# Gate and forget-group weights split during the first feed-forward, a longer reckoned load, and two token blocks per bank

## The chip, the cores and the metric

The kernel runs on one core of a Trainium2 chip. The metric is the device time of one execution in microseconds (us), from three runs of each kernel. The engines are named as the profile names them: PE (TensorE matmul), PEld (TensorE weight load), DVE (VectorE), ACT (ScalarE), POOL (GpSimd) and SP (SyncE, whose queue issues every DMA of this kernel).

## The reference, cut to what matters

One layer on 1024 tokens of width 1024, all in float32: a SwiGLU feed-forward, a mixer of two attentions side by side with sigmoid gates, and a second feed-forward, each behind an RMS norm with a shift, a scale and a gate from a conditioning vector.

```
h = modulate(x, norm_g[l, 0], mod[:, 0, 0], mod[:, 0, 1])
x = x + 0.5 * mod[:, 0, 2][:, None, :] * swiglu(h, ffn1_w1[l], ffn1_w3[l], ffn1_w2[l])
h = modulate(x, norm_g[l, 1], mod[:, 1, 0], mod[:, 1, 1])
# mixer: z = h @ w_in is split into
(fq, fk, fv, ff, dq, dk, dv, iq, ik, iw, ga, gb) = jnp.split(z, split_points, axis=-1)
# FoX: 8 heads, causal softmax with a forget bias; DSA: each query sees its 256 best keys by an index score
merged = jax.nn.sigmoid(ga) * (ya @ w_br_fox) + jax.nn.sigmoid(gb) * (yb @ w_br_dsa)
x = x + mod[:, 1, 2][:, None, :] * (merged @ w_out)
h = modulate(x, norm_g[l, 2], mod[:, 2, 0], mod[:, 2, 1])
x = x + 0.5 * mod[:, 2, 2][:, None, :] * swiglu(h, ffn2_w1[l], ffn2_w3[l], ffn2_w2[l])
```

## The kernel before

**Split operands.** Each float32 operand is split into a high part (ACT copies it to the matmul's type, tile `wh` for weights, `h` for activations) and a low part (the raw tile minus the high part, `wl`), and each product is three matmuls (`mm3`). In the feed-forwards DVE makes the low parts of the weights, as halves of 128x512. In the mixer `load_w` (line 565) loads a raw weight tile `wr` of up to 128x1024, ACT makes `wh`, and POOL (`k.lo_eng`, line 1981) makes `wl`.

**The stages, by the span of the profile.** The first feed-forward's up half (`up_all`, eleven pairs of column blocks, some 130 steps of twelve matmuls) ends near 470 us and its down half near 690; the normed `h` and the index, key and value projections follow; from 705 to 840 the index scores and the first two forget groups of the FoX attention (`fox_group`: query, key and value of two heads). From 840 to 1045 PE computes, one after the other, forget group 2, some gate columns, forget group 3, gates, the query groups `dq_group` 0, gates, `dq_group` 1 and the rest of the gates, while DVE and ACT run `topk` beside it: a search bit by bit for each query's 256th best score, with counts on DVE (`tkj`) and sign tests on ACT (`tks`), each depending on the last. From 1045 to 1405 the attentions run, with the gates of the second token half and the first branch products as filler. From 1405 on come branches, output projection and the second feed-forward, until 2229.

**The gates.** `gates` (line 1072) takes the 16 weight tiles `w_g[b]` (128x1024) for one half of the tokens; it runs twice, so each tile is loaded, copied by ACT and subtracted by POOL twice. `Ahead` (line 1054) holds the weights loaded in advance, three tiles in the stage from 840, one later. Their buffers come from `Ring`s: five pairs `wh`/`wl` and three raw tiles, and in the attentions two pairs and two raw tiles.

**The wide groups.** Forget groups 2 and 3 and both query groups run `group` with `wide`: weight tile by weight tile, and within each over all eight token blocks of 128, so eight accumulations are open at once, each in its own PSUM bank. `chain8` (line 62) deals these banks: four halves of the two 128x1024 tiles `p2`, then four tiles `pj`. The gates use the same four `pj`. At the end of a group ACT copies each block out (`qkv<-p`, `qkv<-pj`), 128x384 for a forget group and 128x256 for a query group.

**What sets the order.** `Plan` records each stage's instructions and `flush` writes them out engine by engine, by reckoned start times: each engine takes, of its ready tasks, the one that can start first, by rank. A task that is meant to fill gaps gets its rank raised (`nc.behind`). A load is reckoned to be there 0.7 us after its bytes are through the wire (lines 394 and 395):

```
self.wire = max(self.wire, s + 1.3) + t.bytes / 345e3
end = self.wire + 0.7
```

On the chip each engine then runs its own instructions strictly in that order.

Of the kernel before, what the change touches and what calls it, by code (L numbers as in the profile page):

```python
# [204 lines left out]
class Plan:  # L205
# [116 lines left out]
    def flush(self, keep=()):  # L322
# [42 lines left out]
        while len(order) < len(tasks):  # L365
# [180 lines left out]
class Ring:  # L546
# [416 lines left out]
def group(k, src, n, ptile, wide, done, weight=1.9):  # L963


    if not wide:
# [8 lines left out]
    ps = []  # L975
    for i in range(4):
        hi, lo = next(src)
        for tk in range(8):
            if i == 0:
                ps.append(ptile())  # L980
            hf, o = tk // 4, (tk % 4) * 128
            for c in range(2):
                hh, hl = (t[hf][2 * i + c][:, o:o + 128] for t in (k.hh, k.hl))
                cs = slice(c * n, c * n + n)
                mm3(k, ps[tk][:, :n], hh, hl, hi[:, cs], lo[:, cs], i + c == 0, i == 3 and c == 1)
            if i == 3:
                done(tk, ps[tk])
# [13 lines left out]
def norm_group(k, p, tmp, src, n, ptile, wide, weight=1.9):  # L1001
# [4 lines left out]
    def done(tk, ps):  # L1006
        k.nc.scalar.activation(t[tk // 4][:, tk % 4, :], ps[:, :n], AF.Copy)
# [934 lines left out]
def layer(tc, xT, c, pos, ada_w, ada_b, ng, inv, w13a, w2a, w_a, w_f, w_q, w_g, fb, fg, dg, wbr, wout, w13b, w2b, out):  # L1942
    with ExitStack() as es:
# [38 lines left out]
        dram = lambda shape, nm: dp.tile(shape, F32, name=nm)  # L1982
# [16 lines left out]
        with ExitStack() as ph:  # L1999
# [24 lines left out]
            def consts():  # L2024
# [15 lines left out]
                yield  # L2040

# [78 lines left out]
            for i in range(2, head):  # L2120
# [3 lines left out]
                if i == 4:  # L2124
# [12 lines left out]
            rest = up_all(k, pairs, head, [], {2: [more], 4: [more], 6: [more]}, lambda: down.loads(down.LEAD), chain(consts(), rest),  # L2137
                          (nc.vector, nc.vector), True, lambda n: n % 2)
            steps = {(5, 4): [lambda: stats(0)]}
# [7 lines left out]
            for q in range(4 * PAIRS):  # L2147
                steps.setdefault(divmod(q, PAIRS), []).append(more_mod)
            down.run(steps)
            assert next(rest, None) is None  # L2150
# [51 lines left out]
        with ExitStack() as ph:  # L2202
# [16 lines left out]
            for i, (w, n) in enumerate(((w_f[2], 768), (w_f[3], 768), (w_q[0], 512), (w_q[1], 512))):  # L2219
                parts += [(w[j], n, r5) for j in range(4)] + [(w_g[b], D, r5) for b in range(3 * i, 3 * i + 3)]  # L2220
            ws = Ahead(k, parts + [(w_g[b], D, r5) for b in range(12, 16)] + [(w_g[b], D, r2) for b in range(2)], 3)
# [5 lines left out]
        with ExitStack() as ph:  # L2227
            tp = pool(ph, "topk", True)
            pj = lambda: pq.tile([128, H], F32, tag="pj", name="pj", bufs=4)
            bank8 = chain8(pj, p2)  # L2230
            gt = gates(k, ws, 0, tp, pj, 2)
# [178 lines left out]
```

## Time and profile before

| | us |
|---|---|
| three runs, median (lowest to highest) | 2230.95 (2229.25 to 2231.05) |
| the profiled execution | 2230.78 |
| its span, first to last instruction | 2229.0 |
| PE busy | 2166.7 (97%) |
| DVE busy | 1638.6 (74%) |
| ACT busy | 1145.2 (51%) |
| POOL busy | 252.0 (11%) |

The profiled execution lies 1.8 us above its span. PE's busy time is modelled; a matmul of 128x512 takes its turn every 0.233 us when nothing holds it. The granted TensorE clock is 0.994 of full speed over the span, the rest lies in a few short stretches at half. DMA moved 315.88 MB, at a mean of 142 GB/s.

### The profile page before, as it was taken

To read this page: it belongs to the slowest core of one execution; us is meant where nothing else is said; L and a number is where in the kernel's file an instruction comes from. 1 tells how busy PE (TensorE), PEld (TensorE's weight loads), DVE (VectorE), ACT (ScalarE), POOL (GpSimd) and SP (SyncE) were. 2 spreads that over 40 slices of the span, in tenths; PEclk is the share of its full clock that TensorE was granted. 3 is DMA by queue.
4 is the path that set the end of the run, shared out by engine and by line. 5 is a ranking of instruction groups with operands and counts; after the bars stand their busy time and mean duration, and the time that the engine had idled before them with its cause. 6 is when DMAs were issued, how large, how long until landed. Compare 5 with 4: busy or idle time off the path is not lost.

```text
span 2229.0 us, 31185 instructions
## 1 busy us (share of the span) xinstructions
PE 2166.7 (97%) x10700; PEld 1782.9 (80%) x10700; DVE 1638.6 (74%) x3095; ACT 1145.2 (51%) x2105; POOL 252.0 (11%) x225
## 2 busy tenths in 40 slices
PE   7999999999999999989999998999999999999999
PEld 5877788887889899977777777777778888888887
DVE  7968776688684698888887677498865755558665
ACT  5634433444464566787777677244443333334443
POOL 0000000000010222223445343000000000000000
PEclk9999999999999999999999999999999999999999
DMA  9245543695421323235232212596224443258520
GB/s 333 95 149 178 173 152 109 213 351 195 125 89 57 109 78 130 96 123 161 90 120 88 72 39 81 202 354 189 66 81 132 137 130 103 96 207 287 166 76 38
DMA packets 186267, 315.88 MB, mean 142 GB/s; under 512 B 27238, under 2 KB 51814, under 8 KB 186108
## 3 DMA queue, kind: packets, MB, share of 16 engines
q1 hardware_dynamic: 186108, 313.89, 42.4%
q8 instruction: 84, 1.38, 0.3%
q14 instruction: 75, 0.61, 0.1%
HBM read 237.53 MB, written 76.28 MB: 141 GB/s over the span
## 4 chain that ended last, share of the span: by engine, by line
PE 82%; DVE 8%; ACT 5%; DMA 3%; issue 2%; SPq 0%; POOL 0%; DVEq 0%; ACTq 0%; POOLq 0%
PE bs L425 34%; PE b L425 28%; PE py L425 7%; PE pj L425 6%; PE p L425 5%; PE pt L425 2%; DVE qkv L425 1%; ACT tks L425 1%; DVE xc L425 1%; DMA mraw<-in_ada_w 1%; DMA wr<-in_w_f 1%; ACT pth L425 1%; ACT pr L425 1%; ACT wh L425 1%; DVE wl L425 1%
## 5 line engine op out<-in xcount | busy, mean ns | idle before, releaser
L425 PE MATMUL bs<-h,wh 128*128 128x512 f32 x1728 | 543.0, 395 | 1.6 <-ACT bs L425 1.3
L425 ACT ACTIVATE wh<-wr 128x512 fp32r<-128x512 f32 (+2 forms) x366 | 246.5, 679 | 451.7 <-PE bs L425 208.3
L425 PEld LDWEIGHTS bs<-h,wh 128*128 128x128 f32 x1728 | 322.9, 188 | 81.9 <-ACT bs L425 5.7
L425 PE MATMUL b<-h,wh 128*128 128x512 f32 x1088 | 344.8, 397 | 5.7 <-ACT z L425 2.6
L425 PE MATMUL bs<-h,wl 128*128 128x512 f32 x864 | 338.7, 393 | 0.5 <-DVE wl L425 0.5
L425 DVE TENSOR_TENSOR wl<-wr,wh 128x512 fp32r<-128x512 f32 x308 | 205.4, 686 | 123.5 <-ACT wh L425 116.6
L425 PEld LDWEIGHTS b<-h,wh 128*128 128x128 f32 x1088 | 205.0, 189 | 55.5 <-ACT z L425 3.5
L425 PE MATMUL b<-h,wl 128*128 128x512 f32 x544 | 214.7, 395 | 0.1
L425 PEld LDWEIGHTS bs<-h,wl 128*128 128x128 f32 x864 | 162.2, 188 | 39.2 <-DVE wl L425 0.9
L425 ACT ACTIVATE wh<-a 128x512 fp32r<-128x512 f32 x132 | 83.3, 631 | 174.4 <-PE b L425 93.0
L425 POOL TENSOR_TENSOR wl<-wr,wh 128x1024 fp32r<-128x1024 f32 (+2 forms) x58 | 123.8, 2137 | 328.6 <-ACT wh L425 323.3
L425 DVE TENSOR_TENSOR wl<-a,wh 128x512 fp32r<-128x512 f32 x132 | 91.3, 692 | 88.1 <-ACT wh L425 83.5
L425 PE MATMUL b<-wh 128*128 128x512 f32 x352 | 137.2, 390 | 0.7 <-ACT mrow L425 0.7
L425 PE MATMUL b<-wh,wl 128*128 128x512 f32 x352 | 137.0, 389 | 0.0
L425 PE MATMUL b<-wl,wh 128*128 128x512 f32 x352 | 137.0, 389 | 0.0
L425 PE MATMUL pj<-wh,h 128*128 128x384 f32 (+1 forms) x512 | 125.8, 324 | 0.3 <-ACT wh L425 0.2
L425 PEld LDWEIGHTS b<-h,wl 128*128 128x128 f32 x544 | 102.8, 189 | 25.1 <-DVE wl L425 0.7
L425 DVE TENSOR_TENSOR z<-bs,z 128x512 f32<-128x512 f32 x116 | 79.3, 687 | 58.7 <-PE bs L425 36.8
L425 POOL TENSOR_SCALAR pr<-pr,mn 128x128 f32<-128x128 f32 (+7 forms) x128 | 100.0, 801 | 134.7 <-DVE mn L425 127.5
L425 DVE TENSOR_TENSOR wl<-g,wh 128x512 fp32r<-128x512 f32 x154 | 106.5, 694 | 2.5 <-ACT wh L425 2.5
L425 ACT ACTIVATE pr<-pr,mn 128x256 f32<-128x256 f32 (+7 forms) x128 | 98.4, 770 | 18.0 <-DVE mn L425 17.7
L425 PE MATMUL bs<-wl,wh 128*128 128x512 f32 x264 | 103.1, 391 | 2.1 <-DVE wl L425 1.9
(322 smaller groups left out, 4405.2 us busy)
## 6 DMA issues: line engine op xcount, KB each, us to landing
d_g<-z SPq DMA_DIRECT2D x154, 256.0 KB, 2.1
g<-d_g SPq DMA_DIRECT2D x154, 256.0 KB, 4.7
mraw<-in_ada_w SPq DMA_DIRECT2D x144, 256.0 KB, 5.3
wr<-in_w13a SPq DMA_DIRECT2D x112, 256.0 KB, 5.3
wr<-in_w13b SPq DMA_DIRECT2D x88, 256.0 KB, 4.6
wr<-in_w_g SPq DMA_DIRECT2D x32, 512.0 KB, 4.2
a<-in_w2a SPq DMA_DIRECT2D x44, 256.0 KB, 5.1
a<-in_w2b SPq DMA_DIRECT2D x44, 256.0 KB, 5.3
```

Of the source, the lines that this page charges most:

```text
L425: getattr(getattr(self.tc.nc, e), t.op)(*map(real, t.a), **{n: real(v) for n, v in t.kw.items()})
```

## The change

1. `parts()`, new in the first feed-forward: 40 pieces (four weight tiles of forget group 2 in halves of 128x384, the 16 gate tiles in halves of 128x512). For each piece, one DMA loads it (`gw`), ACT makes the high part, POOL the low part, and two DMAs write both parts to DRAM (`d_wf..`, `d_wg..`). The 80 half-steps are hung on `up_all`'s steps 30 to 125, with ranks raised by 200.
2. Where the mixer needs these weights, `load_w` loads the high and the low part straight into the pair `wh`, `wl`: two DMAs, no raw tile, no ACT, no POOL. This holds for forget group 2 and for the gates, both times. Pairs are now dealt in turn.
3. The planner reckons a load 1.0 us longer.
4. `dq_group` takes its banks from `chain4`: only the four halves of the two `p2` tiles. Two token blocks of 256 columns share a bank, so a group has four accumulations of 128x512 and four copies out instead of eight.

```diff
+def chain4(two):
+    while True:
+        t = two()
+        yield t[:, 0:H]
+        yield t[:, H:T]
...
-                end = self.wire + 0.7
+                end = self.wire + 1.7
...
-        return tuple(p.tile([128, D], F32R, tag=t, name=t, bufs=n) for t in ("wh", "wl"))
+        return tuple(p.tile([128, D], F32R, tag=t, name=t, bufs=n, in_turn=True) for t in ("wh", "wl"))
...
+    if isinstance(src, tuple):
+        t = k.w.pair()
+        for part, d in zip(t, src):
+            nc.sync.dma_start(part[:, :n].bitcast(F32), d)
+        return t
...
-    ps = []
+    ps, m = [], H // n
...
-            if i == 0:
+            if i == 0 and tk % m == 0:
                 ps.append(ptile())
...
-                mm3(k, ps[tk][:, :n], hh, hl, hi[:, cs], lo[:, cs], i + c == 0, i == 3 and c == 1)
-            if i == 3:
-                done(tk, ps[tk])
+                mm3(k, ps[tk // m][:, tk % m * n:tk % m * n + n], hh, hl, hi[:, cs], lo[:, cs], i + c == 0,
+                    i == 3 and c == 1, tk % m > 0)
+            if i == 3 and tk % m == m - 1:
+                done(tk, ps[tk // m])
...
+            def parts():
+                for src, dst in todo:
+                    n = dst[0].shape[1]
+                    m = n if n <= H else n // 2
+                    for c in range(0, n, m):
+                        nc.behind = 200
+                        t, hi, lo = (t512(k, dt, "gw")[:, :m] for dt in (F32, F32R, F32R))
+                        nc.sync.dma_start(t, src[:, c:c + m])
+                        nc.scalar.activation(hi, t, AF.Copy)
+                        nc.gpsimd.tensor_sub(lo, t, hi.bitcast(F32))
...
+                        for d, x in zip(dst, (hi, lo)):
+                            nc.sync.dma_start(d[:, c:c + m], x.bitcast(F32))
...
+            for n in range(80):
+                steps.setdefault(30 + 96 * n // 80, []).append(lambda: next(gw, None))
...
-                       dq_group(k, fp, fp, tp, ws, 0, lambda: next(bank8), 0.8), islice(gt, 15),
-                       dq_group(k, fp, fp, tp, ws, 1, lambda: next(bank8), 0.6), gt)
+                       dq_group(k, fp, fp, tp, ws, 0, lambda: next(bank4), 0.8), islice(gt, 15),
+                       dq_group(k, fp, fp, tp, ws, 1, lambda: next(bank4), 0.6), gt)
```

In the order of the program, the kernel before: PE where query group 0 ends and the gates follow. `pj` on the left is a bank that is written, `wh,h` its weight and activation operands; `p_9157` and `p_9163` are the two `p2` tiles of query group 1.

```order
L425 MATMUL pj<-wl,h 128x256
L425 MATMUL pj<-wh,h 128x256
L425 MATMUL p_9157<-wh,h 128x256 x2
L425 MATMUL p_9163<-wh,h 128x256 x2
L425 MATMUL pj<-h,wh 128x512 x2
L425 MATMUL pj<-h,wl 128x512
```

The same place in the changed kernel; `p_9305` is the second `p2` tile of query group 0.

```order
L433 MATMUL p_9305<-wh,h 128x256 x2
L433 MATMUL p_9305<-wl,h 128x256
L433 MATMUL p_9305<-wh,h 128x256
L433 MATMUL pj<-h,wh 128x512 x2
L433 MATMUL pj<-h,wl 128x512
```

The gates' first bank (`pj<-h,wh 128x512`) no longer is a bank that the query group has just filled, and the four early matmuls of the next group have gone from between.

ACT at that place, before: the sign tests (`tks`) and the copies out of query group 0.

```order
L425 ACTIVATE qkv<-p_8674 128x256
L425 ACTIVATE tks,tksgn<-tkh_7948,tkca 128x896
L425 ACTIVATE qkv<-p_8674 128x256
L425 ACTIVATE tks,tksgn<-tkh_7920,tkca 128x768
L425 ACTIVATE fsq<-qkv 128x512
L425 ACTIVATE qkv<-p_8872 128x256 x2
L425 ACTIVATE qkv<-pj 128x256 x4
```

And in the changed kernel:

```order
L433 ACTIVATE qkv<-p_9086 128x512
L433 ACTIVATE tks,tksgn<-tkl_8308,tkca 128x768
L433 ACTIVATE fsq<-qkv 128x512
L433 ACTIVATE qkv<-p_9086 128x512
L433 ACTIVATE tks,tksgn<-tkl_8370,tkca 128x1024
L433 ACTIVATE qkv<-p_9305 128x512
L433 ACTIVATE tks,tksgn<-tkl_8338,tkca 128x896
L433 ACTIVATE fsq<-qkv 128x512
```

Sign tests still stand between the copies, but no copy out of a `pj` is left among them.

SP in the first feed-forward, before: the loads of one pair's weights (`wr`) between those for the conditioning rows (`mraw`); `d_g` is a store of the feed-forward.

```order
L425 DMA mraw<-in_ada_w 128x512 x2
L425 DMA d_g_120<-z 128x512
L425 DMA mraw<-in_ada_w 128x512 x2
L425 DMA wr<-in_w13a 128x512 x2
L425 DMA mraw<-in_ada_w 128x512
L425 DMA wr<-in_w13a 128x512 x2
```

The same four `wr` loads in the changed kernel and what now stands ahead of them (`gw` is a piece, `d_wg3h` and the like are the parts written out):

```order
L433 DMA d_wg3l<-gw 128x512
L433 DMA d_wg3h<-gw 128x512
L433 DMA mraw<-in_ada_w 128x512
L433 DMA d_wg3l<-gw 128x512
L433 DMA mcol<-d_row_163 128x4x1
L433 DMA d_wg4h<-gw 128x512
L433 DMA d_wg4l<-gw 128x512
L433 DMA gw<-in_w_g 128x512
L433 DMA d_g_200<-z 128x512
L433 DMA d_wg4h<-gw 128x512
L433 DMA wr<-in_w13a 128x512 x4
```

The four loads have moved behind stores that wait for ACT and POOL.

## Rows read from the trace of the kernel before

**Rows 1.** The page's first part: busy us, share of the span, instructions.

```profile
PE 2166.7 (97%) x10700; PEld 1782.9 (80%) x10700; DVE 1638.6 (74%) x3095; ACT 1145.2 (51%) x2105; POOL 252.0 (11%) x225
```

**Rows 2.** Windows by stage: stretch, us; PE, PEld, DVE, ACT, POOL busy; clock, DMA share, GB/s.

```profile
195.00:490.00 295.00, 294.03 (x1267) 235.87 (x1266) 215.14 (x342) 114.90 (x200) 0.00 (x0) 1.00 0.58 195
705.00:840.00 135.00, 127.30 (x726) 121.54 (x724) 90.94 (x160) 71.54 (x121) 31.72 (x24) 1.00 0.28 90
840.00:1045.00 205.00, 197.21 (x1108) 176.30 (x1108) 170.06 (x505) 159.30 (x293) 56.16 (x28) 0.98 0.37 118
1045.00:1405.00 360.00, 342.64 (x2346) 273.87 (x2345) 275.59 (x609) 255.49 (x557) 151.93 (x157) 0.98 0.30 93
```

**Rows 3.** Waits of PE: engine and tile, what it waited for, us, times, longest.

```profile
PE p L425 <- ACT ir L425: 4.6, 4, 1.9
PE p L425 <- ACT qkv L425: 4.3, 5, 1.5
PE pj L425 <- ACT qkv L425: 3.5, 1, 3.5
...
PE pt L425 <- DMA nat<-d_qkv: 1.3, 1, 1.3
```

**Rows 4.** Timeline of PE: start, us, instruction, [idle before <-releaser].

```profile
949.07 0.50 PE L425 MATMUL p<-wh,h 128*128 128x256 f32 x2 [1.05 <-ACT qkv L425]
951.05 0.51 PE L425 MATMUL p<-wh,h 128*128 128x256 f32 x2 [1.48 <-ACT qkv L425]
...
995.58 0.72 PE L425 MATMUL pj<-h,wh 128*128 128x512 f32 x2 [3.52 <-ACT qkv L425]
```

**Rows 5.** Timeline of ACT, 993 to 996 us.

```profile
994.01 1.15 ACT L425 ACTIVATE tks<-tkl,tkca 128x1024 bf16<-128x1024 uint16 x1
...
995.14 0.39 ACT L425 ACTIVATE qkv<-pj 128x256 f32<-128x256 f32 x1
```

**Rows 6.** Windows as in group 2, of shorter stretches.

```profile
230.00:260.00 30.00, 29.71 (x127) 23.38 (x126) 27.96 (x45) 12.12 (x21) 0.00 (x0) 1.00 0.51 167
430.00:510.00 80.00, 79.32 (x346) 64.22 (x345) 62.76 (x103) 37.65 (x67) 0.00 (x0) 1.00 0.96 339
946.00:956.00 10.00, 7.47 (x35) 6.11 (x34) 7.64 (x21) 9.69 (x22) 1.39 (x2) 0.83 0.16 50
990.00:1000.00 10.00, 6.48 (x30) 5.38 (x29) 8.32 (x31) 10.00 (x24) 1.83 (x2) 0.83 0.66 201
```

**Rows 7.** Timeline of DVE and of POOL near 932 us.

```profile
932.04 0.15 DVE L425 TENSOR_TENSOR tku<-tkcnt,tklim 128x3 uint32<-128x3 f32 x1
932.23 2.26 DVE L425 SCALAR_TENSOR_TENSOR tkkey<-tku,tkkey 128x3 uint32<-128x3 uint32 x1
...
932.07 2.40 POOL L425 TENSOR_TENSOR wl<-wr,wh 128x1024 fp32r<-128x1024 f32 x1 [3.16 <-ACT wh L425]
```

**Rows 8.** Groups of DVE, 840 to 1045 us: xcount | busy, mean ns | idle before.

```profile
L425 DVE TENSOR_TENSOR qkv<-qkv,fnr 128x1024 f32<-128x1024 f32 x10 | 16.0, 1643 | 0.1
L425 DVE TENSOR_TENSOR tku<-tkcnt,tklim 128x3 uint32<-128x3 f32 x32 | 11.7, 365 | 0.8
L425 DVE TENSOR_TENSOR tkv<-tksgn,tklim 128x3 f32<-128x3 f32 x31 | 11.2, 361 | 19.8 <-ACT tks L425 19.7
L425 DVE TENSOR_TENSOR qkv<-qkv,g_dq 128x1024 f32<-128x1024 f32 x4 | 4.9, 1216 | 0.0
```

**Rows 9.** Groups of POOL, 840 to 1045 us.

```profile
L425 POOL TENSOR_TENSOR wl<-wr,wh 128x1024 fp32r<-128x1024 f32 x16 | 38.5, 2404 | 95.0 <-ACT wh L425 95.0
L425 POOL TENSOR_TENSOR wl<-wr,wh 128x512 fp32r<-128x512 f32 x8 | 10.3, 1292 | 45.3 <-ACT wh L425 45.3
```

**Rows 10.** Groups of ACT: the first of 195 to 490 us, the second of 840 to 1045.

```profile
L425 ACT ACTIVATE wh<-wr 128x512 fp32r<-128x512 f32 x76 | 47.7, 630 | 111.7 <-PE bs L425 63.9 <-PE b L425 35.0 <-issue 6.6
...
L425 ACT ACTIVATE wh<-wr 128x1024 fp32r<-128x1024 f32 x16 | 16.9, 1054 | 10.9 <-issue 10.9
```

**Rows 11.** Page, DMA issues: count, KB each, median us from issue to landing.

```profile
wr<-in_w_g SPq DMA_DIRECT2D x32, 512.0 KB, 4.2
```

More of the change, by code (lines that the diff above doesn't have):

```diff
@@ L1006, in done @@
     def done(tk, ps):
-        k.nc.scalar.activation(t[tk // 4][:, tk % 4, :], ps[:, :n], AF.Copy)
+        m = H // n if wide else 1
+        k.nc.scalar.activation(t[tk // 4][:, tk % 4 - m + 1:tk % 4 + 1, :], ps[:, :m * n].rearrange("p (a b) -> p a b", a=m),
+                               AF.Copy)
         if tk % 2:
@@ L1981, in layer @@
         k.lo_eng = nc.gpsimd
-        dram = lambda shape, nm: dp.tile(shape, F32, name=nm)
+        dram = lambda shape, nm, dt=F32: dp.tile(shape, dt, name=nm)
+        split_in = lambda n, m, nm: [tuple(dram([128, m], f"d_{nm}{i}{x}") for x in "hl") for i in range(n)]
+        d_wg = split_in(16, D, "wg")
+        d_wf = [split_in(4, 768, f"wf{i}") for i in range(4)]
+        d_wq = [split_in(4, 512, f"wq{i}") for i in range(2)]
+        todo = [(w[i], d[i]) for w, d in (((w_f[2], d_wf[2]), (w_g, d_wg))) for i in range(len(d))]
         d_x = dram([8, 128, T], "d_x")
@@ L2040, in consts @@
                 yield
+            def parts():
[8 more added lines that the diff above has]
+                        nc.gpsimd.tensor_sub(lo, t, hi.bitcast(F32))
+                        nc.behind = 0
+                        yield
+                        nc.behind = 200
+                        for d, x in zip(dst, (hi, lo)):
+                            nc.sync.dma_start(d[:, c:c + m], x.bitcast(F32))
+                        nc.behind = 0
+                        yield
             sq1 = [SquareSum(k, nc.vector), SquareSum(k, nc.vector)]
@@ L2136, in layer @@
             more()
-            rest = up_all(k, pairs, head, [], {2: [more], 4: [more], 6: [more]}, lambda: down.loads(down.LEAD), chain(consts(), rest),
+            gw = parts()
+            steps = {2: [more], 4: [more], 6: [more]}
+            for n in range(80):
+                steps.setdefault(30 + 96 * n // 80, []).append(lambda: next(gw, None))
+            rest = up_all(k, pairs, head, [], steps, lambda: down.loads(down.LEAD), chain(consts(), rest),
                           (nc.vector, nc.vector), True, lambda n: n % 2)
+            assert next(gw, 0) == 0
             steps = {(5, 4): [lambda: stats(0)]}
@@ L2148, in layer @@
                 steps.setdefault(divmod(q, PAIRS), []).append(more_mod)
+            for q in range(0, 0):
+                steps.setdefault(divmod(q, PAIRS), []).append(lambda: next(gw, None))
             down.run(steps)
-            assert next(rest, None) is None
+            assert next(rest, None) is None and next(gw, 0) == 0
             nc.flush([t for r in down.x for t in r] + [t for r in wa for t in r] + k.hh[0] + k.hl[0] + [a.acc for a in sq1])
@@ L2218, in layer @@
             parts = []
-            for i, (w, n) in enumerate(((w_f[2], 768), (w_f[3], 768), (w_q[0], 512), (w_q[1], 512))):
-                parts += [(w[j], n, r5) for j in range(4)] + [(w_g[b], D, r5) for b in range(3 * i, 3 * i + 3)]
-            ws = Ahead(k, parts + [(w_g[b], D, r5) for b in range(12, 16)] + [(w_g[b], D, r2) for b in range(2)], 3)
+            for i, (w, n) in enumerate(((d_wf[2], 768), (w_f[3], 768), (w_q[0], 512), (w_q[1], 512))):
+                parts += [(w[j], n, r5) for j in range(4)] + [(d_wg[b], D, r5) for b in range(3 * i, 3 * i + 3)]
+            ws = Ahead(k, parts + [(d_wg[b], D, r5) for b in range(12, 16)] + [(d_wg[b], D, r2) for b in range(2)], 3)
             nc.flush(k.hh[0] + k.hl[0] + k.hh[1] + k.hl[1] + [t for w in ws.q for t in w])
@@ L2230, in layer @@
             bank8 = chain8(pj, p2)
+            bank4 = chain4(p2)
             gt = gates(k, ws, 0, tp, pj, 2)
```

2 lines of the change are left out of this document (1 added, 1 removed).

## The prediction, made before the changed kernel ran

> **What bounds the kernel now.** I read the page's first part, then windows by stage, then PE's waits, then the timeline at the longest of them. The page shows PE busy for 2166.7 of 2229.0 us [rows 1], so 62.3 us of idle PE is all that a change without fewer matmuls can take away, beside some stretches at a lower clock. Nearly no matmul is removed here, so the forecast is a sum over PE's gaps. The windows tell where they lie [rows 2]: 0.97 us of idle PE in the first feed-forward from 195 to 490 us (295.00 less 294.03), 7.70 in the index stage, 7.79 in the stage of groups and gates from 840 to 1045, 17.36 in the attentions. In the third of these ACT is busy 159.30 of 205 us and DVE 170.06, so PE there waits for engines that are themselves full. Of PE's waits by name, those for ACT's copies out of a bank (qkv) make 4.3 and 3.5 us [rows 3]. The timeline shows the three longest of them [rows 4]: 1.05 us at 949.07 and 1.48 us at 951.05, where query group 0 has ended, and 3.52 us at 995.58, where query group 1 has ended and the first gate matmul wants a bank pj. All four pj hold the query group, and ACT comes to the first of them at 995.14, behind a sign test of 1.15 us at 994.01 [rows 5]. So it is not the copy that is slow (0.39 us); it stands behind the search in ACT's row.
>
> After both places the granted clock is 0.83 over ten microseconds [rows 6]. As the levels are full and half (2.4 and 1.2 GHz), 0.17 x 10 / 0.5 = 3.4 us ran at half and gave up 1.7 us of matmul time, each time behind idle PE.
>
> **Part 4, two blocks per bank.** The query groups no longer touch pj. In the order of the changed kernel the gates' first matmul follows the group's last one in a bank that was free all the while, so the wait at 995.58 goes whole: 3.52 us. The waits at 949.07 and 951.05 are those of the next query group's first matmuls, which the planner had drawn forward into a place where nothing else could run; they are now behind 72 gate matmuls, and these have banks: 1.05 + 1.48 us more. With the idle time the two half-clock stretches should go: 2 x 1.7 us. Sum: 3.52 + 2.53 + 3.4 = 9.45 us. Bounds: all of it, or 3.5 us if ACT's other copies (the forget groups still fill pj) keep one of the two stretches alive. I take 9.5, since the row at 995.58 names the bank and the order shows it gone. ACT's copies fall from 16 of 128x256 to 8 of 128x512, a microsecond or two of ACT in 205; I count nothing for that. What is late next there are the p2 banks: they must be copied out before the next query group, but 72 gate matmuls at 0.233 us, 16.8 us, lie between, and in the order the four copies take their places within ten rows of ACT.
>
> **Part 2, weights loaded ready.** From 840 to 1045 ACT loses 16 copies (16.9 us) [rows 10] and POOL 16 subtractions (38.5 us) [rows 9]; four more of each, of 128x768, go before 840, and 16 each in the attentions. POOL itself is on no path of PE's. But its subtractions hold DVE up: a three-element DVE instruction that takes 0.15 us at 932.04 takes 2.26 us at 932.23, while POOL subtracts from 932.07 for 2.40 [rows 7]. Over the stage this cost DVE about 17 us: 32 x (0.365 - 0.155) + 31 x (0.361 - 0.155) + 10 x (1.643 - 1.216) = 6.7 + 6.4 + 4.3 [rows 7, 8], beside 56.2 us of busy POOL [rows 2], or 0.31 us per us. Most of it goes. That shortens the search, which PE does not wait for by itself, so I count it at nothing in this stage beyond the 9.5. In the index stage PE's waits for ACT (ir) are 4.6 us in four [rows 3]; ACT and POOL are relieved of four splits there; I take 1 us, between 4.6 and a loss of 2 from the new order. In the attentions ACT is relieved of 16 x 1.054 = 16.9 us of 255 [rows 2, 10]; PE's 17.4 us of gaps there are chains of transpose, copy and product, to which that is 7% of ACT's load; 7% of 17.4 is 1.2, and I take 1, between 5 of gain and 5 of loss. The price of this part is that a gate's weights are now 1 MB of DMA instead of 0.5, issued when a pair comes free; a 512 KB load lands after 4.2 us [rows 11]. Three tiles are held ahead, and each is 24 matmuls or 5.6 us of PE: 16.8 us against some 6 to 8. I count nothing; without that lead it would be a microsecond or two per tile.
>
> **Part 1, the pieces.** It adds, from about 195 to 490 us, 40 copies on ACT (40 x 0.63 = 25 us on top of 114.9 of 295), 40 subtractions on POOL (32 x 1.292 + 8 x 0.97, scaled by width = 49.1 us, where POOL was idle), and 120 DMAs on SP: 32 x 0.75 MB and 8 x 0.56 MB, 29 MB, so some 97 GB/s on top of 195, where a DMA share of 0.96 goes with 339 GB/s: the share rises from 0.58 to some 0.85 [rows 2, 6, 9, 10]. PE has 0.97 us to gain there and so can nearly only lose. What can make it lose is DVE, which feeds it the low parts. At 0.31 us per us of POOL, DVE loses 15 us of 295, and 215 becomes 230: it has room on the mean. In stretches it has none: from 230 to 260 it is busy 27.96 of 30 us [rows 6]. If the delay of those 30 of 295 us reaches PE, it is 49.1 x 30 / 295 = 5.0 us with every microsecond of POOL counted, 1.5 at the rate of the search stage. I take 3, between the two, and as bounds -1 (the idle PE there) and 5.
>
> The Trainium skill, "SBUF — State Buffer", section "Who interferes with whom", speaks against this part: a DVE instruction with both inputs in SBUF and a GpSimd one that reads SBUF exclude each other for the whole instruction, and the second to come is fully blocked. The trace agrees for [rows 7]; by that rule DVE in the first feed-forward, where nearly all instructions have two SBUF inputs, could lose the full 49 us and stand at 264 of 295, and this term of the sum would be 5 instead of 3.
>
> The other thing that can lose is the place where the pieces end: from 430 to 510 us DMA is already 0.96 busy [rows 6], and the order has the last pieces among the first loads of the down half. They lead by several steps, so I count it in the 3.
>
> **Part 3, the longer reckoning.** It changes no instruction, only the planner's order. PE's order is unchanged up to some 200 us, in nearly all of the first down half, and from 1552 us to the end; it differs between. The one wait of PE that ends with a DMA is 1.3 us [rows 3], so I take 0, within 2 either way.
>
> **Sum.** -9.5 - 1 - 1 + 3 = -8.5 us. On the profiled execution, 2230.78 - 8.5 = 2222.3; its median of runs is 2230.95, the same within 0.2, so I predict **2222.3 us**.
>
> **The rivals.** *(a) The waits move, and little is gained.* The gate weights come straight into their pair, behind whatever SP waits for, and PE waits for DMA instead of for banks. For it: two DMAs per tile in an in-order queue, and in the attentions a lead of one tile only. Against it: the lead of three before, and attention work between the gates after. If 32 gate passes wait 0.25 us each, 8 us come back: 2222.3 + 8 = 2230, the time of before. It decides from a lead below about 8 us. *(b) Slower: POOL's subtractions starve PE in the first feed-forward.* Place: the pairs between 195 and 470 us. Mechanism: DVE held per piece by up to 1.29 us, low parts of the weights late, and SP's loads of the next pair (now behind stores that wait for POOL) late as well. Price: if the whole 15 us of delayed DVE reaches PE, 2230.8 - 11.5 + 15 = 2234; if two fifths of POOL's 49 us do, 2239. It decides from 11.5 us on, where it has eaten the gain; then DVE must have no slack at all in 295 us, and it has 27% now. *(c) More is gained.* With POOL off DVE and ACT relieved, the other gaps shrink too: beside the 9.5 go the rest of the 7.8 (1.7), a third of the 17.4 in the attentions (5.8) and the index stage's 4.6, and 3 are lost in the first feed-forward: 2230.8 - 18.6 = 2212; with half of these extras 2218. For it: ACT is busy 255 of 360 us in the attentions [rows 2]; against it: the order of the attentions hardly changes, and their gaps end with ACT and DVE work that stays. That the change doesn't do what it says is excluded by the order: no query group writes a pj, and no ACT or POOL split of a gate is left in the mixer.
>
> **How the numbers follow.** Forecast 0.50 (2218 to 2226), rival (a) 0.23 (2226 to 2234), rival (b) 0.15 (2233 to 2242), rival (c) 0.12 (2211 to 2218). The likeliest is 2222.3. A range from 2214 to 2236 leaves out the ends of (b) and (c), some 0.15. This kernel's runs can tell about 0.2%, 4.5 us, from no change: below 2226.5 is faster, above 2235.4 slower. Faster: 0.50 + 0.12 and little of (a), less the upper edge of the forecast, 0.61. Slower: most of (b), 0.14, and a little of (a), 0.02, 0.16. Same: the rest, 0.23.
>
> **What would show it.** Right: after both query groups gate matmuls follow without idle PE, no clock below 1.00 there, PE busy above 203 of the 205 us; POOL's busy time about 40 us in the first feed-forward, DVE above 225 of the 295, and PE idle there below 5. Part 2 shows in the small DVE instructions of the search, back near 0.2 us on the mean. Wrong: PE's waits in the first feed-forward for wl or wh of more than 8 us, or waits of gate matmuls for DMA wh or wl. If the stage of groups and gates is not some 9 us shorter, the term of part 4 is wrong; if it is and the time is not, part 1 has eaten it.

## The result, and the profile after

The changed kernel takes **2208.1 us** (median of 4 runs, 2207.09 to 2209.04) against 2230.67 (2229.25 to 2231.05) for the kernel before beside it: a ratio of 0.990, interval 0.9883 to 0.9917. That is 22.6 us less, where 8.5 were forecast, and below the range.

The profiled execution has a span of 2205.4 us. First its engines (busy us, share, instructions), which answer to [rows 1]:

```profile
PE 2159.9 (98%) x10700; PEld 1777.8 (81%) x10700; DVE 1639.2 (74%) x3095; ACT 1133.7 (51%) x2101; POOL 222.1 (10%) x229
```

Idle PE went from 2229.0 - 2166.7 = 62.3 us to 2205.4 - 2159.9 = 45.5, that is 16.8 less. PE's busy time fell by another 6.8 us with the same 10700 matmuls, which fits the clock: it stood at half for 27.9 us of the span before and for 10.2 us after. 16.8 + 6.8 = 23.6, the whole difference of the spans. The windows that answer to [rows 2] (engine: busy us and count; PE's granted clock, DMA share, GB/s):

```profile
195.00:490.00 295.00, 293.13 (x1259) 234.47 (x1258) 230.84 (x325) 131.60 (x236) 56.03 (x40) 1.00 0.81 275
705.00:840.00 135.00, 131.09 (x750) 125.65 (x749) 90.86 (x191) 73.32 (x125) 17.11 (x18) 1.00 0.35 119
840.00:1045.00 205.00, 201.90 (x1166) 179.94 (x1164) 159.72 (x518) 150.53 (x289) 24.63 (x22) 1.00 0.51 175
1045.00:1405.00 360.00, 347.86 (x2358) 278.91 (x2359) 272.34 (x585) 239.24 (x526) 112.46 (x134) 1.00 0.38 123
```

The granted clock reads 1.00 in all four, 0.98 stood in two of them. But the same microseconds no longer hold the same work, so from here on stages are cut at PE's own instructions. *First part*: up to the first matmul into a `pj` of the projections. *Index*: up to the first `p<-wh,h`, forget group 2. *Groups*: up to the first attention product `p<-qs`. *Attentions*: up to their last product. *Rest*. The kernel before:

```profile
0.00:723.24 723.24, 704.56 (x3093) 570.58 (x3094) 545.01 (x927) 336.05 (x583) 15.87 (x19) 1.00 0.51 171
723.24:822.03 98.79, 91.09 (x530) 86.05 (x529) 72.33 (x123) 63.97 (x112) 20.21 (x20) 1.00 0.27 90
822.03:1038.16 216.13, 208.34 (x1171) 188.58 (x1169) 183.95 (x528) 157.33 (x287) 61.54 (x30) 0.98 0.36 116
1038.16:1402.99 364.83, 347.48 (x2378) 277.94 (x2378) 277.74 (x621) 260.23 (x565) 154.33 (x158) 0.98 0.30 92
```

and the changed one, with the same count of matmuls in each:

```profile
0.00:724.09 724.09, 706.55 (x3093) 570.48 (x3094) 570.57 (x927) 355.30 (x624) 71.61 (x58) 1.00 0.63 212
724.09:818.66 94.57, 90.67 (x530) 85.97 (x529) 68.74 (x126) 62.37 (x108) 13.42 (x16) 1.00 0.31 107
818.66:1024.51 205.85, 203.90 (x1171) 186.24 (x1169) 170.09 (x540) 146.17 (x271) 18.05 (x12) 1.00 0.48 165
1024.51:1380.48 355.97, 343.67 (x2378) 275.29 (x2378) 269.04 (x605) 241.85 (x540) 119.04 (x143) 1.00 0.37 118
```

First part +0.9 us, index -4.2, groups -10.3, attentions -8.9, rest -1.1. The stage on which the forecast staked 9.5 us did gain 10.3, as the forecast's own sign of being right asks ("some 9 us shorter"). That was luck: the runs show that the reason given for it was false.

PE's waits from 705 to 1405 us, the answer to [rows 3] (us in total, times, longest):

```profile
PE py L433 <- DVE ptl L433: 4.4, 11, 1.2
PE p L433 <- DVE mn L433: 2.7, 5, 0.9
PE p L433 <- ACT ir L433: 2.5, 3, 1.4
PE p L433 <- ACT qkv L433: 2.0, 3, 0.7
```

The waits for `qkv` fell from 4.3 + 3.5 us to 2.0, the one for `pj` among them is gone, and in this kernel no wait of PE ends with a DMA.

### The profile page after: what moved, and what is told of

It reads as the page before. It is cut to its first block, busy times and chain, and to the rows that moved or that the text cites. A ratio compares the mean times of both kernels' runs of the same rounds, so it can differ in the third digit from the quotient of the medians.

```text
span 2205.4 us, 31519 instructions
## 1 busy us (share of the span) xinstructions
PE 2159.9 (98%) x10700; PEld 1777.8 (81%) x10700; DVE 1639.2 (74%) x3095; ACT 1133.7 (51%) x2101; POOL 222.1 (10%) x229
## 3 DMA queue, kind: packets, MB, share of 16 engines
q1 hardware_dynamic: 208572, 362.13, 49.1%
## 4 chain that ended last, share of the span: by engine, by line
PE 86%; DVE 6%; ACT 3%; DMA 2%; issue 2%; SPq 0%; POOL 0%; DVEq 0%; ACTq 0%; POOLq 0%
PE bs L433 34%; PE b L433 28%; PE pj L433 7%; PE py L433 7%; PE p L433 7%; PE pt L433 3%; DVE xc L433 1%; DVE macc L433 1%; ACT pr L433 1%; DVE wl L433 1%; ACT pth L433 1%; DVE xb L433 1%; DVE ptl L433 0%; SPq L433 0%; DMA gw<-in_w_f 0%
## 5 line engine op out<-in xcount | busy, mean ns | idle before, releaser
L433 ACT ACTIVATE wh<-wr 128x512 fp32r<-128x512 f32 (+1 forms) x330 | 207.3, 638 | 359.0 <-PE bs L433 166.9
L433 DVE TENSOR_TENSOR z<-bs,z 128x512 f32<-128x512 f32 x116 | 79.4, 687 | 48.2 <-PE bs L433 27.7
L433 DVE SCALAR_TENSOR_TENSOR macc<-mraw,cond,macc 128x512 f32<-128x512 f32 x119 | 96.5, 811 | 10.4 <-DMA mraw<-in_ada_w 8.6
L433 PE MATMUL pj<-wh,h 128*128 128x384 f32 x384 | 102.8, 338 | 0.0
```

What stands on the lines that cost most here:

```text
L433: getattr(getattr(self.tc.nc, e), t.op)(*map(real, t.a), **{n: real(v) for n, v in t.kw.items()})
```

## The experiments

Each kernel below was timed beside the kernel before, at some 2229 to 2231 us; the ratio and its interval are against that. Stage lengths are from the one profiled execution of each, in brackets the idle PE plus the matmul time lost at half clock. How many half-clock stretches of 3.4 us (1.7 us lost each) a stage has differs by one or two between kernels that have the same order there, so differences below 3 us in one stage are not read. In `pool_back` and `pool_first` a gate tile of 24 matmuls (5.6 us) lies behind the cut between groups and attentions: beside the other rows their groups are 5.6 us longer than they stand here, and their attentions as much shorter.

```
kernel           median  ratio (interval)         first part   index       groups       attentions
before           2230.7                           723 (20.4)   98.8 (7.7)  216.1 (11.2) 364.8 (24.2)
changed          2208.1  0.990 (0.9883, 0.9917)   724 (19.2)   94.6 (3.9)  205.8 (2.0)  356.0 (14.0)
p4_only          2232.1  1.0007 (0.9996, 1.0017)  727 (24.0)  102.4 (11.8) 215.8 (10.7) 362.0 (21.2)
p3_only          2222.1  0.996 (0.9947, 0.9977)   722 (18.6)  103.3 (13.6) 211.9 (7.4)  358.8 (18.0)
p12_only         2223.5  0.997 (0.9955, 0.9976)   739 (32.5)   97.4 (6.4)  203.1 (0.0)  358.3 (18.2)
no_p3            2223.9  0.997 (0.9959, 0.9989)   738 (32.9)   97.2 (6.4)  205.1 (1.4)  358.8 (18.8)
no_p4            2207.8  0.991 (0.9891, 0.9924)   725 (18.6)   94.9 (4.3)  206.0 (2.5)  355.8 (13.7)
no_p12           2220.5  0.996 (0.9947, 0.9977)   722 (19.1)  102.9 (14.0) 211.4 (7.3)  357.4 (14.5)
no_p2            2222.0  0.997 (0.9954, 0.9979)   725 (19.5)  103.1 (13.5) 212.2 (8.3)  357.8 (15.9)
act_back         2208.5  0.991 (0.9888, 0.9921)   724 (19.0)   94.6 (3.6)  207.7 (4.2)  356.2 (13.5)
pool_back        2232.9  1.0011 (1.0000, 1.0021)  726 (19.7)   98.2 (8.3)  208.8 (11.0) 374.6 (23.9)
pool_first       2225.2  0.997 (0.9959, 0.9984)   725 (18.8)   98.4 (8.6)  209.0 (11.1) 367.9 (19.1)
raw_hf1          2208.1  0.990 (0.9883, 0.9913)   724 (18.8)   97.5 (7.0)  205.9 (2.0)  356.5 (13.9)
nosub_no_p3      2211.8  0.991 (0.9880, 0.9943)   727 (22.0)   94.5 (3.7)  205.1 (1.4)  355.8 (14.4)
dve_no_p3        2222.6  0.995 (0.9936, 0.9970)   737 (32.1)   97.4 (6.3)  205.1 (1.4)  355.3 (13.4)
dve_no_p4        2210.6  0.990 (0.9885, 0.9920)   729 (24.2)   94.8 (4.2)  206.4 (2.9)  356.0 (13.7)
lag_no_p3        2225.4  0.998 (0.9961, 0.9990)   746 (40.1)   96.5 (5.8)  205.1 (1.4)  355.3 (13.5)
lag_no_p4        2210.2  0.990 (0.9877, 0.9924)   726 (21.1)   95.0 (4.3)  206.1 (2.6)  356.2 (14.0)
w27              2218.5  0.994 (0.9929, 0.9959)   735 (28.0)   98.2 (7.8)  206.9 (2.5)  354.0 (11.7)
all_down         2225.5  0.998 (0.9970, 0.9989)   740 (34.4)   95.5 (4.9)  206.8 (3.1)  355.7 (13.7)
```

### One part alone

**Part 4 alone** (the query groups take their banks from `chain4`, all else as before).

> The kernel before with part 4 alone (two token blocks per bank in the query groups). All theories: the stage from the first matmul of forget group 2 to the first attention product, 216.1 us before and 205.9 in the changed kernel, takes 206 to 208. Theory R (relief: the attentions gained because ACT and POOL lost their splits): the attentions stay at their 364.8 us within 2, the time is 2230.7 - 9.5 = 2221. Rival O (order: the longer reckoning of loads re-placed the work there): the same. Rival S (shift: a shorter stage of groups alone lets the search end earlier and the attentions start unhindered): attentions 357 to 361, time 2214 to 2217.

Nothing is gained: the groups take 215.8 us where every theory had 206 to 208. The wait for `pj` at 995.58 [rows 4] is gone, as forecast, and the wait stands at the next bank instead. PE in this kernel (start, us, in brackets the idle time before and what ended it):

```profile
955.44 0.39 PE L433 MATMUL p<-wh,h 128*128 128x256 f32 x1 [3.45 <-ACT qkv L433]
999.19 0.39 PE L433 MATMUL p<-wl,h 128*128 128x256 f32 x1 [2.84 <-ACT qkv L433]
```

The second of them, followed back through ACT, DVE and POOL of the same kernel:

```profile
998.56 0.58 ACT L433 ACTIVATE qkv<-p 128x512 f32<-128x512 f32 x1
...
995.18 1.15 ACT L433 ACTIVATE tks<-tkl,tkca 128x1024 bf16<-128x1024 uint16 x1 [2.07 <-DVE tkca L433]
...
994.92 0.17 DVE L433 TENSOR_SCALAR tkca<-tkkey 128x3 f32<-128x3 f32 x1
...
993.15 1.54 DVE L433 TENSOR_TENSOR tkv<-tksgn,tklim 128x3 f32<-128x3 f32 x1 [0.30 <-ACT tks L433]
...
992.28 2.39 POOL L433 TENSOR_TENSOR wl<-wr,wh 128x1024 fp32r<-128x1024 f32 x1 [5.09 <-ACT wh L433]
```

POOL subtracts from 992.28 to 994.67. A three-element DVE step of the search that takes 0.16 us undisturbed lasts until 994.69. The next trial value `tkca` is late, ACT's sign test waits 2.07 us for it, three sign tests stand ahead of the copy in ACT's row, and PE waits for the copy. The same chain was in the kernel before, some ten microseconds ahead of the 3.52 us wait on which the forecast rested (there the held step also stands behind multiplications of DVE's own that end near 982):

```profile
981.89 2.40 POOL L425 TENSOR_TENSOR wl<-wr,wh 128x1024 fp32r<-128x1024 f32 x1 [3.24 <-ACT wh L425]
...
981.93 2.38 DVE L425 TENSOR_TENSOR tkv<-tksgn,tklim 128x3 f32<-128x3 f32 x1
...
984.80 1.15 ACT L425 ACTIVATE tks<-tkl,tkca 128x1024 bf16<-128x1024 uint16 x1 [2.99 <-DVE tkca L425]
```

**Part 3 alone** (loads reckoned 1 us longer).

> The kernel before with part 3 alone (loads reckoned 1 us longer). Theory R: attentions 364.8 within 2, index stage 98.8 within 1.5, time 2231 within 3. Rival O: the attentions take 357 to 360 and the index stage 95 to 96, time 2220 to 2223. Rival S: as R.

8.2 us less. Rival O had the time and the attentions (358.8 us), but the index stage got 4.5 us longer and not shorter, and the groups 4.2 us shorter.

**Parts 1 and 2 alone.**

> The kernel before with parts 1 and 2 (weights split in the first feed-forward, loaded ready), neither the longer reckoning nor the wider banks. Theory R: index stage 95 (from 98.8), groups 213 to 216, attentions 356 to 359 (from 364.8), first feed-forward up to 1 us longer; time 2219 to 2223. Rival O: index stage and attentions as before within 2, time 2229 to 2233. Rival S: as O.

The groups, with the old eight banks, have no idle PE at all:

```profile
836.63:1039.75 203.12, 203.12 (x1171) 186.20 (x1170) 170.50 (x539) 144.99 (x270) 18.73 (x12) 1.00 0.50 172
```

So the ready weights take these waits away, not the banks; theory R had 213 to 216 us here. But the first part became 16 us longer, which nobody expected.

### One part undone

Against the changed kernel; `no_p3` first, then `no_p4`, then `no_p2`, where the pieces are made but forget group 2 and the gates load the raw weights again (the second gate line likewise, and pairs no longer in turn). `no_p12` is `no_p2` with no pieces made. The three kernels with one part alone are made of the same edits.

```diff
-                end = self.wire + 1.7
+                end = self.wire + 0.7
...
-                       dq_group(k, fp, fp, tp, ws, 0, lambda: next(bank4), 0.8), islice(gt, 15),
-                       dq_group(k, fp, fp, tp, ws, 1, lambda: next(bank4), 0.6), gt)
+                       dq_group(k, fp, fp, tp, ws, 0, lambda: next(bank8), 0.8), islice(gt, 15),
+                       dq_group(k, fp, fp, tp, ws, 1, lambda: next(bank8), 0.6), gt)
...
-            for i, (w, n) in enumerate(((d_wf[2], 768), (w_f[3], 768), (w_q[0], 512), (w_q[1], 512))):
-                parts += [(w[j], n, r5) for j in range(4)] + [(d_wg[b], D, r5) for b in range(3 * i, 3 * i + 3)]
+            for i, (w, n) in enumerate(((w_f[2], 768), (w_f[3], 768), (w_q[0], 512), (w_q[1], 512))):
+                parts += [(w[j], n, r5) for j in range(4)] + [(w_g[b], D, r5) for b in range(3 * i, 3 * i + 3)]
```

> The changed kernel with loads reckoned as before (part 3 undone). Theory R: 2208 within 3, index stage 94.6 and attentions 355.9 within 2 each. Rival O: attentions 362 to 365, index stage 98, time 2216 to 2221. Rival S: as R.

> The changed kernel with the query groups in the old eight banks (part 4 undone). The prediction's own theory (part 4 takes the waits for banks away): the stage of groups and gates goes from 205.8 back to 214 to 216 us, time 2216 to 2218. Theory D, formed after parts 1 and 2 alone left no idle TensorE in that stage with the old banks (203.1 us): the stage stays at 203 to 206, time 2205 to 2209.

> The changed kernel with the weights split in the mixer as before (parts 1 and 2 undone; parts 3 and 4 stay). Theory D (the splits in the mixer slow the search, and the query groups' copies stand behind it): groups and gates 210 to 214 us, attentions 358 to 362, time 2219 to 2224, as with part 3 alone. The prediction's own theory: groups 206, time 2221 - 8 = 2213 with part 3's own gain.

> The changed kernel that makes and stores the pieces in the first feed-forward but doesn't use them: forget group 2 and the gates split their weights in the mixer as before (part 2 undone). What it is short of the run without parts 1 and 2 is the price of part 1. Theory D: that price is 1 to 3 us in the first feed-forward (up to 725 us), time 2222 to 2226, groups 210 to 214. The prediction's own theory: 3 us of price, groups 206, time 2213 to 2217.

Part 4 undone changes nothing (2207.8), which theory D had and the prediction's own theory had not. Parts 1 and 2 undone cost 12.4 us. Part 3 undone costs 15.8 us, 14 of them in the first part; that kernel's nine executions lie between 2216.9 and 2229.3 us, but `p12_only`, which differs from it in the banks alone, has the long first part too. Making the pieces without using them costs 1.5 us on top of not making them, no more than the executions of one kernel differ.

### Which of the two relieved engines

To the changed kernel an instruction was added for each tile loaded ready, whose result nobody reads: GpSimd's subtraction (`pool_back`, shown; `pool_first` for the first 20 tiles only), or ScalarE's copy of `t[0]` into `raw` (`act_back`).

```diff
             nc.sync.dma_start(part[:, :n].bitcast(F32), d)
+        raw = k.w.raw()
+        nc.gpsimd.tensor_sub(raw[:, :n], t[0][:, :n].bitcast(F32), t[1][:, :n].bitcast(F32))
         return t
```

> The changed kernel with, for each weight tile loaded ready, one subtraction on GpSimd of the old shape added whose result nobody reads (no ScalarE copy is added). Theory P (VectorE held by GpSimd's subtractions made the search late): groups and gates 211 to 216 us again (from 205.8), small VectorE instructions of the search at 0.36 us, time 2215 to 2222. Theory A (ScalarE's copies of the weights did it): groups 206 within 1.5, time 2208 to 2211.

> The changed kernel with, for each weight tile loaded ready, one ScalarE copy of the old shape added whose result nobody reads (no GpSimd subtraction). Theory P (VectorE held by GpSimd's subtractions made the search late): index stage plus groups within 3 of the changed kernel's 300.4 us, attentions 356 to 359, time 2208 to 2214. Theory A (ScalarE's own load did it): index plus groups 306 or more, attentions 361 or more, time 2218 or more.

> The changed kernel with the extra GpSimd subtractions for the first 20 ready tiles only (forget group 2 and the gates' first pass), none in the attentions. Theory P: the search takes 194 to 205 us again (176 in the changed kernel), index stage plus groups 305 to 310 (from 300.4), attentions 358 to 364, time 2217 to 2224. If the dearness of the run with all of them came from the same place: 2228 or more. If the search is not what holds TensorE: 2208 to 2212.

ACT's 36 copies cost 0.4 us, within the spread. POOL's 36 subtractions cost 24.8 us, the 20 beside the search 17.1. The same step in each of the search's 32 rounds, one a bit (ns min/median/max, first and last start in us), in the kernel before, the changed one, with ACT's copies back, with POOL's first 20 back, and in `all_down` (further below), where no weight is split beside the search:

```profile
L425 DVE SCALAR_TENSOR_TENSOR tkkey<-tku,tkkey x32: 154/162/2258, 847.6 to 1041.6; 128x3 uint32<-128x3 uint32 x32
```
```profile
L433 DVE SCALAR_TENSOR_TENSOR tkkey<-tku,tkkey x32: 153/161/165, 835.8 to 1011.8; 128x3 uint32<-128x3 uint32 x32
```
```profile
L433 DVE SCALAR_TENSOR_TENSOR tkkey<-tku,tkkey x32: 153/161/1719, 837.5 to 1013.2; 128x3 uint32<-128x3 uint32 x32
```
```profile
L433 DVE SCALAR_TENSOR_TENSOR tkkey<-tku,tkkey x32: 154/161/164, 844.5 to 1046.1; 128x3 uint32<-128x3 uint32 x32
```
```profile
L433 DVE SCALAR_TENSOR_TENSOR tkkey<-tku,tkkey x32: 152/161/166, 851.8 to 1026.9; 128x3 uint32<-128x3 uint32 x32
```

From first to last 194.0, 176.0, 175.7, 201.6 and 175.1 us. Apart from the two runs with added subtractions, the search takes 194 to 196 us where the gates' first pass is split beside it (before, p4_only, p3_only, no_p12, no_p2) and 174 to 177 where it is ready, whatever else is changed. What goes with this is the time for which POOL holds the search's own DVE instructions (what they take beyond their median without a POOL instruction beside them, summed between these first and last starts):

| kernels | holds on the search's steps, us | search, us |
|---|---|---|
| `all_down` | 0 | 175 |
| first pass ready | 2 to 5 | 174 to 177 |
| first pass split beside the search | 14 to 17 | 194 to 196 |
| `pool_first` | 18.6 | 201.6 |
| `pool_back` | 23.6 | 205.1 |

With `act_back` the search is as short as in the changed kernel, though ACT does 54.0 us of work other than the search's in that time, against 38.8 there and 58.6 in the kernel before.

Both runs came out slower than theory P had it (2215 to 2222 and 2217 to 2224): the added subtractions harm more than those they stand for. They wait in POOL's in-order queue for loads, and in the attentions POOL's own mask work stands behind them. In `pool_back` one such wait of POOL:

```profile
POOL wr L433 <- DMA wl<-d_wg0l: 21.5, 1, 21.5
```

In `pool_first`, which has none in the attentions, the search is still some 7 us longer than with the real subtractions, with 2 to 5 us more of holds on its steps; why they fall there more often was not settled. So these two runs show which engine it is, and overstate how much; the size is the 12.4 us of `no_p12`. How the pairs are dealt was changed together with the ready loads and never by itself.

**The second pass alone split as before** (14 of its 16 tiles, in the attentions; two are loaded earlier and stay ready).

```diff
-        ws.parts, ws.n = [(d_wg[b], D, r2) for b in range(2, 16)] + [(wbr[b], D, r2) for b in range(2)], 1
+        ws.parts, ws.n = [(w_g[b], D, r2) for b in range(2, 16)] + [(wbr[b], D, r2) for b in range(2)], 1
```

> The changed kernel in which the gates' second pass (16 tiles, in the attentions) splits its weights there as before; the first pass and forget group 2 stay ready. If the attentions' gain comes from their own splits: attentions 361 to 365 (from 356.0), time 2214 to 2218, groups unchanged at 206. If it comes mostly from the longer reckoning and from the stage before: attentions 357 to 359, time 2209 to 2212.

No difference: 2208.1 again, and the attentions take 356.5 us, so their gain does not come from their own splits. POOL is busy 32 us more there (151.48 us against 119.04), and that costs nothing. The DVE instructions of that stage, first in the changed kernel, then in this one (busy us, mean ns):

```profile
L433 DVE TENSOR_TENSOR ptl<-pt,pth 128x512 fp32r<-128x512 f32 x96 | 65.0, 687 | 22.0 <-ACT pth L433 21.7
```
```profile
L433 DVE TENSOR_TENSOR ptl<-pt,pth 128x512 fp32r<-128x512 f32 x96 | 64.4, 685 | 24.1 <-ACT pth L433 23.8
```

`pt` is a bank, so they read SBUF with one operand only, and POOL holds none of them up. This agrees with the Trainium skill, "SBUF — State Buffer", section "Who interferes with whom", by which a DVE instruction with at most one SBUF input, outside the two-port modes, doesn't contend with GpSimd. So 14 of the 36 ready tiles bring nothing.

### Why part 1 needs part 3

In the first part POOL holds DVE for 27.7 us in the changed kernel and 27.8 in `no_p3` (summed over the DVE instructions that overlap one of POOL's: their time beyond the median of the same instruction without overlap). The one loses nothing by it, the other 14 us. What differs is DVE's waits for DMA from 195 to 490 us; the changed kernel, then `no_p3`:

```profile
DVE macc L433 <- DMA mraw<-in_ada_w: 7.8, 7, 2.3
DVE wr L433 <- DMA wr<-in_w13a: 5.0, 3, 3.7
```
```profile
DVE wr L433 <- DMA wr<-in_w13a: 14.6, 8, 3.5
DVE macc L433 <- DMA mraw<-in_ada_w: 11.0, 10, 2.2
```

> Part 3 undone, and each piece of the first feed-forward loaded a step (some 3.5 us) before its ScalarE copy instead of in the same step. Without part 3 that stage took 737.9 us (724.1 in the changed kernel). Theory W (ScalarE's copies stand waiting for loads that have not landed, and hold the rows behind them): 724 to 728, time 2209 to 2213. Theory L (VectorE held by GpSimd's subtractions): 736 to 740, time 2220 to 2226. Theory T (the traffic and the buffers of the pieces): the same as L.

> Part 3 undone, and the pieces' subtractions left out: their high part is stored in the place of the low one, so that this part of the computation is missing; ScalarE's copies and all DMAs stay. Theory L: the first feed-forward takes 723 to 727 us (737.9 with them), VectorE there 28 us less held, time 2208 to 2212. Theory W or T: 734 to 739, time 2218 to 2224.

> Part 3 undone and the pieces' subtractions on VectorE. Without part 3 the first feed-forward took 737.9 us with them on GpSimd and 726.6 with none. If 28 us more of VectorE's time there are too much by themselves: 734 us or more, time 2218 or more. If the harm came from locks that fall at other places than the order reckons with: 724 to 729, time 2208 to 2214.

The edits, against `no_p3`: in `lag_no_p3` the load of piece i + 1 is issued with the stores of piece i; in `dve_no_p3` the pieces' subtraction is on DVE; in `nosub_no_p3` that line is left out and `hi` stored twice.

```diff
                             nc.sync.dma_start(d[:, c:c + m], x.bitcast(F32))
+                        load(i + 1)
...
-                        nc.gpsimd.tensor_sub(lo, t, hi.bitcast(F32))
+                        nc.vector.tensor_sub(lo, t, hi.bitcast(F32))
```

The earlier load hardly shortened ACT's waits for pieces (38.5 us, 42.2 in `no_p3`), and the first part got longer still (746 us, in no theory's range), so that run by itself says little of theory W; but the changed kernel has 32.2 us of them and `nosub_no_p3` 30.3, and lose nothing by it. Without the subtractions the stage came back to 726.6 us, although DVE waited as long for DMA as before:

```profile
DVE wr L433 <- DMA wr<-in_w13a: 16.3, 10, 3.3
DVE macc L433 <- DMA mraw<-in_ada_w: 12.1, 10, 3.8
```

So it is the subtractions, as theory L has it. Leaving them out also freed a buffer and spared SP's row its waits for POOL (19.3 us in `no_p3`), but DVE's waits for loads did not fall by that. With the same subtractions on DVE itself the stage took 736.7 us, which speaks for the amount and against the places where the holds fall (though DVE there also waits 18.8 us for ACT's copies of pieces). Either burden alone fits into DVE's slack: 31.2 us of DMA waits in all and no holds (726.6), or 27.7 us of holds with 13.5 of waits (724.1). Both together, 27.8 + 29.5, don't: 737.9. `p12_only` (27.1 + 28.0: 739.2), `lag_no_p3` (24.9 + 33.2: 745.6) and `lag_no_p4` (21.1 + 20.9: 726.2) agree; that the sum decides is a reading of these runs, and where DVE's slack ends no run measured. In `no_p3` PE waits for `z`:

```profile
PE bs L433 <- DVE z L433: 7.8, 6, 2.8
```

### Versions that might be better

```diff
-                end = self.wire + 1.7
+                end = self.wire + 2.7
...
-        todo = [(w[i], d[i]) for w, d in (((w_f[2], d_wf[2]), (w_g, d_wg))) for i in range(len(d))]
+        todo = [(w[i], d[i]) for w, d in (((w_f[2], d_wf[2]), (w_f[3], d_wf[3]), (w_q[0], d_wq[0]), (w_q[1], d_wq[1]), (w_g, d_wg))) for i in range(len(d))]
...
-            for q in range(0, 0):
+            for q in range(0, 32):
```

The first is `w27`, the others are `all_down` (which also loads these groups ready and has the old eight banks); `dve_no_p4` and `lag_no_p4` are the edits above beside the old eight banks.

> A further kernel: the changed one with the old eight banks, and the weights of forget group 3 and both query groups split ahead too (16 more pieces of 128x384 and 128x512, put into the first feed-forward's down half). Theory P: no split of a weight is left in the mixer after the projections, VectorE runs free in the search; index plus groups 297 to 299 (from 300.4), first feed-forward 724 to 727, time 2203 to 2207. Against: the down half loses as much to GpSimd as the mixer gains, time 2208 to 2212.

> The changed kernel with loads reckoned another 1 us longer (2.7 us after the wire). If the gain of part 3 is that work no longer stands before a load that has not landed, and 1.7 is near what loads take: 2206 to 2210. If the reckoning was still short: 2202 to 2205. If longer waits only hold buffers: 2211 or more.

> A further kernel: the changed one with the old eight banks and the pieces' 40 subtractions on VectorE instead of GpSimd. On GpSimd each of them cost VectorE 27.7 / 40 = 0.69 us in the first feed-forward, as much as a subtraction of 128x512 takes on VectorE itself. If this lock is the whole price, VectorE is as busy as before in that stage (231 of 295 us) and the time is 2205 to 2210. If VectorE's row, which runs in order, now stands behind pieces that have not landed: 2212 or more.

> A further kernel: the changed one with the old eight banks and each piece loaded a step before its copy. Theory W: ScalarE's 32 us of waits for pieces shrink, but TensorE waits only some 1 us there by now: 2206 to 2209. Others: the same.

None beats the changed kernel. With 16 more pieces in the down half PE waited up to 4.9 us for `wh` and `wl` around 535 us, the first part lost 15 us, and the three stages of the mixer gained nothing (658.0 us against 656.7 in `no_p4`): with the last 12 splits gone from beside it the search takes 175.1 us against 176.6. At 2225.5 us the kernel lies in neither range. Of the three reckonings tried 1.7 is the best: at 2.7 the first part lost 11 us again. With the pieces' subtractions on DVE itself the kernel takes 2210.6 us, with the earlier load 2210.2, against 2207.8 in `no_p4`; both lie just above the lower range that was expected for them.

## Why the prediction was wrong, step by step

- **Part 4, -9.45: false.** The step that failed is "the row at 995.58 names the bank and the order shows it gone". It is gone, and alone it brings +1.8 us (interval -0.9 to 3.8); undone, it costs nothing. The copy stood behind the search, whatever bank it empties. The reading stopped at the sign test of 1.15 us in ACT's row [rows 5]. That test waited for nothing; ACT's row is full from 984.80 on, and the reading did not follow it back to the test there, which had waited 2.99 us for a DVE step that POOL held. The counter, "What is late next there are the p2 banks", was named and dismissed; they made waits of 3.45 and 2.84 us.
- **Part 2, the shorter search, "which PE does not wait for by itself, so I count it at nothing": false.** The forecast had the mechanism and most of its size (17 us of DVE held by three groups of instructions; all of DVE's together were held 24.3 us from 840 to 1045) [rows 7, 8], and priced it at nothing. PE does wait for the search, through ACT's row. It is worth 12.4 us in the changed kernel, most of it in groups and index stage: 211.4 + 102.9 against 205.8 + 94.6. ACT's relief, which the forecast counted in the attentions, is worth nothing there.
- **Part 1, +3 in the first feed-forward: inside its bounds, but not by its working.** The first part became 0.9 us longer; the medians of `no_p2` and `no_p12` differ by 1.5. DVE lost 27.7 us there, not 15: POOL worked 56.0 us and not 49.1, and DVE lost 0.49 us per us of it instead of 0.31. The forecast named both burdens on DVE apart, never their sum; without part 3 the term would have been 14 to 16 us, so that it came out small is luck.
- **Part 3, 0 within 2: false.** -8.2 alone, -15.8 on top of the others. "The one wait of PE that ends with a DMA is 1.3 us" looked at PE; the DMA waits that count are DVE's.
- **Attentions, -1 within 5: mis-sized**, -8.9. Idle PE fell by 5.1 us and PE's busy time by 3.8, the latter with the clock: four half-clock stretches of 3.4 us (two at 1051, one each at 1068 and 1368 us) became one. The forecast priced such stretches after the query groups and left these out. Parts 3 alone and 1 and 2 alone each bring about 6 here. The cause is not settled. Their own splits are excluded (`raw_hf1`), and a search that ends earlier can't be all of it: with part 3 alone it still takes 194.6 us.
- **Index stage, -1 within -4.6 to +2:** -4.2, inside the bounds. Part 3 alone made it 4.5 us longer, with ready weights it didn't.
- **The rivals.** (a) did not come: no PE wait ends with a DMA. (b) is a real mechanism, POOL's subtractions starving PE through DVE, and without part 3 it does cost 14 to 16 us in the first part, its own number; even then the kernel was faster than before (2223.9), not at (b)'s 2234. (c), POOL off DVE and the other gaps smaller too, came nearest in mechanism and time (2212): the index stage's 4.6 us were 4.2, the attentions' 5.8 were 8.9, and the loss of 3 in the first feed-forward was 0.9. But it too took the 9.45 for the banks' doing, and counted ACT's relief.
- **The parts do not add up.** Parts 1 and 2 alone -6.9, part 3 alone -8.2, part 4 alone +1.8, together -13.3; the change brings -22.6. The missing 9 lie where parts are harmful alone (parts 1 and 2 by 16 us in the first part, part 3 by 4.5 in the index stage, part 4 by 4 in each of the two), less what several of them gain alone and the change only once (by the stages some 7 us in the groups, 6 in the attentions, 4 in the rest).

## What to carry to other kernels

Follow a wait back until the chain reaches an engine that worked all the while, through rows of other engines too: a copy that stands behind other work gains nothing from another bank if that work is itself held. Before moving work to a relieved engine's idle stretch, add up everything that its neighbour there must bear (its own work, the holds, its waits for DMA); two burdens that each fit may not fit together. And a reckoning of loads is a part of the change like any other: here it turned a loss of 14 us in the first part into none.

## What the runs showed of the hardware

- The 40 subtractions of pieces on POOL (32 of 128x512 with a median of 1.30 us, 8 of 128x384), beside DVE work mostly with two SBUF operands, cost DVE 27.7 us, 0.69 us each; one of 128x512 on DVE itself takes 0.69 us undisturbed. On POOL they relieved DVE of next to nothing.
- Beside DVE instructions with one operand in a bank, 14 POOL subtractions of 2.3 us cost nothing that could be measured.
- The search's large comparisons, one SBUF operand of up to 640 elements, kept their 0.88 us at most beside POOL (27 of the 96 in the kernel before overlap one of its subtractions), while three-element instructions with two operands rose from 0.16 to 2.38.
- One operand alone does not protect: `tkca<-tkkey`, a three-element instruction with one SBUF operand and a median of 0.17 us, rose to 2.38 us beside a POOL subtraction (`p3_only`, `no_p12`, `no_p2`).
